# Triangular inverses from blocks of 8 instead of blocks of 16, with a product level from 8 to 16

## The chip, the cores and the metric

One core of a Trainium2 chip. The metric is the device time of one execution in microseconds. TensorE (PE) multiplies, VectorE (DVE), ScalarE (ACT) and GpSimd (POOL) work elementwise, SyncE (SP) issues most DMAs. Each engine works through its own queue in order.

## What is computed

Two layers of a recurrent decoder trunk on 1024 prompt rows and 8 x 8 sample rows of width 1024, in float32. Layer 0 mixes with an S5 scan and a gated DeltaNet (GDN, 4 heads of 128), layer 1 with RWKV-7 (16 heads of 64); each layer ends in a SwiGLU network of width 2816. What matters here is that GDN and RWKV are computed in chunks, and that each chunk needs the inverse of a unit triangular matrix:

```python
lmat = jnp.where(strict, jnp.einsum("nbhid,nbhjd->nbhij", k_beta, kb) * decay, 0.0)
eye = jnp.eye(CHUNK, dtype=jnp.float32)
tmat = lax.linalg.triangular_solve(eye + lmat, jnp.broadcast_to(eye, lmat.shape),
                                   left_side=True, lower=True)
...
state = (state * w_t[:, :, None, :] + sa[..., None] * b_t[:, :, None, :]
         + v_t[..., None] * k_t[:, :, None, :])
```

The RWKV recurrence is written step by step in the reference; the kernel computes it in chunks of 64, which brings in an inverse of the same kind.

## The kernel before, in words

The rows stand in the free dimension (1088 = 1024 + 64 columns), the features in the partitions. All large products go through `Kern.mm` (L293 to L302): operands are split into a high and a low part, and three products per 128 features are summed (`hi,wh`, `lo,wh`, `hi,wl`). `Kern.weight` (L280) loads a weight block as `raw`, casts it on ScalarE (`wh`, L289) and subtracts on GpSimd (`wl`, L290) or, in places, on VectorE. The feed-forward network (`Kern.ffn`, L456) makes products `pg` (gate and up) and `pd` (down); VectorE evicts them (L490, L496, L498, and L513, which adds to the residual `x`).

Between these dense products the program places the two recurrent mixers, which are made of small products and many elementwise steps:

- `GDN.segment` (L966): 4 heads, each in two segments, 8 calls. A call has 4 chunks of 128, the second segment also the 8 samples.
- `RWKV.unit` (L1517): 8 pairs of heads, each in 4 segments, 32 calls. A call has 4 chunks of 64 for two heads; the fourth segment a fifth for the samples.

Each call needs one batch of inverses, made by `Kern.inverse` (L141 to L257), 40 in all. It works in this order:

1. VectorE multiplies the 256 or 320 columns of the matrices with a mask (`mk`, L158) and adds up (`D`, L160), so that the 16x16 blocks on the diagonal stand next to each other. Two DMAs through DRAM (`dA`, L161 and L165) put each block into one partition (`L`).
2. Substitution: starting from the identity (`T`, L167), 15 steps of two instructions each, a product `Tm` (L172) and a subtraction or addition into `T` (L174), on 32 to 40 partitions and 15 to 64 elements.
3. Two DMAs (`dT`, L176 and L178) bring the inverted blocks back as columns `Tc`. A mask and a 32x32 transpose make `tt` and `t32` (L189, L194).
4. Level 16 to 32: two groups of 32x32 products with 16 columns, L202 and L206, with a ScalarE copy between (`Y`, L203) and a multiply-add at the end (L208), then a transpose (L212).
5. Level 32 to 64: two more groups (L230, L238) and copies; for GDN one more level from 64 to 128.

The order of the instructions on every engine is written by a scheduler that works from a model of its own when the program is built; the code gives data dependences and priorities. The units are thereby interleaved with dense products and with each other.

Of the kernel before, what the change touches and what calls it, by code (L numbers as in the profile page):

```python
# [8 lines left out]
F32 = mybir.dt.float32  # L9
# [3 lines left out]
OP = mybir.AluOpType  # L13
# [4 lines left out]
T = 1088  # L18
# [72 lines left out]
class Kern:  # L91
    def __init__(self, ctx, tc):
# [23 lines left out]
        def blocks(n, w, name):  # L116
# [7 lines left out]

        self.b16 = blocks(8, 16, "b16")
        self.b8 = blocks(16, 8, "b8")
        self.m4 = c.tile([128, 4], F32, name="m4")
        nc.vector.tensor_add(self.m4, self.b16[:, 0:4], self.b16[:, 4:8])
# [6 lines left out]
        ii = c.tile([128, 16, 16], F32, name="ii")  # L135
        nc.gpsimd.iota(ii, pattern=[[1, 16], [-1, 16]], base=0, channel_multiplier=0,
                       allow_small_or_imprecise_dtypes=True)
        nc.vector.tensor_scalar(ii, ii, 0.0, None, op0=OP.is_equal)
        self.i16 = ii

    def inverse(self, gp, ps, dr, A, wd, nu, ns, sgn, tag, pb=2, own=False, TT=None):  # L141

# [1 line left out]


        nc, v = self.nc, self.nc.vector
        nl = 8 * nu + ns
        op = OP.subtract if sgn > 0 else OP.add
        dA = dr.tile([nu + 1, 8, 256], F32, name="dA", tag="dA%d" % wd)
        size = {"mk": 320, "L": 256, "T": 256, "tt32": 160, "Y32": 160}  # L150
        kin = {"Y32": "L", "tt32": "T"}
        two = [lambda n, i=i: gp.tile([128, size[kin.get(n, n)] if own else 320], F32, name=n,
                                      tag="i" + kin.get(n, n) if own else "inv%d" % i, bufs=1) for i in range(2)]
        D = gp.tile([128, nu + 1, 16], F32, name="D", tag="invTc", bufs=1 + own)
        for R, n in ((slice(0, 64), nu + 1 if ns else nu), (slice(64, 128), nu)) if wd == 128 else ((slice(0, 128), nu),):
            mk = two[1]("mk").rearrange("p (u b i) -> p u b i", b=4, i=16)[R, 0:n]
# [4 lines left out]
        nc.sync.dma_start(dA[0:nu].rearrange("u b (j i) -> (b j) u i", i=16), D[:, 0:nu])  # L161
        if ns:
            nc.sync.dma_start(dA[nu, 0:ns].rearrange("b (j i) -> (b j) i", i=16), D[0:16 * ns, nu])
        L = two[0]("L")[:8 * nu + 8, :256].rearrange("p (a b) -> p a b", b=16)
        nc.sync.dma_start(L[:nl], dA.rearrange("u b (j i) -> (u b) j i", i=16)[:nl])  # L165
        T = two[1]("T")[:8 * nu + 8, :256].rearrange("p (a b) -> p a b", b=16)
        v.tensor_copy(T[:nl], self.i16[:nl])  # L167
        m = gp.tile([8 * nu + 8, 64], F32, name="Tm", tag="invm", bufs=1)
# [6 lines left out]
        dT = dr.tile([nu + 1, 8, 256], F32, name="dT", tag="dT%d" % wd)  # L175
        nc.sync.dma_start(dT.rearrange("u b x -> (u b) x")[:nl], T[:nl].rearrange("p c i -> p (c i)"))  # L176
        Tc = gp.tile([128, nu + 1, 16], F32, name="Tc", tag="invTc", bufs=1 + own)
        nc.sync.dma_start(Tc[:, 0:nu], dT[0:nu].rearrange("u b (c i) -> (b c) u i", i=16))  # L178
        TS = None
        if ns:  # L180
            R = 16 * ns
            nc.sync.dma_start(Tc[0:R, nu], dT[nu, 0:ns].rearrange("b (c i) -> (b c) i", i=16))
            TS = gp.tile([R, 4, 16], F32, name="TS", tag="invTS", bufs=1)
            v.tensor_mul(TS, Tc[0:R, nu:nu + 1].to_broadcast([R, 4, 16]),
                         self.m4[0:R, :, None].to_broadcast([R, 4, 16]))
            TS = TS.rearrange("p b i -> p (b i)")

        tt = gp.tile([128, nu, 2, 16], F32, name="tt", tag="invtt", bufs=1)
        v.tensor_mul(tt, Tc[:, 0:nu, None].to_broadcast([128, nu, 2, 16]),  # L189
                     self.half[:, None, :, None].to_broadcast([128, nu, 2, 16]))  # L190
        t32 = gp.tile([128, nu, 32], F32, name="t32", tag="invt32", bufs=1)
        fl = lambda x: x.rearrange("p u c -> p (u c)")
        tt = tt.rearrange("p u a i -> p u (a i)")
        v.transpose(fl(t32), fl(tt))  # L194
        Q = [slice(32 * b, 32 * b + 32) for b in range(4)]
        C = [slice(32 * b % wd, 32 * b % wd + 32) for b in range(4)]
        CT = Q
        Y = gp.tile([128, nu, 16], F32, name="Y16", tag="invY", bufs=1)
        py = ps.tile([128, 2, nu, 16], F32, tag=tag, name="py", bufs=pb)
        for u in range(nu):  # L200
# [6 lines left out]
        k = 1 if sgn > 0 else 0  # L207
# [977 lines left out]
class RWKV:  # L1185
# [32 lines left out]
    def consts(self, cp):  # L1218

        K, v = self.K, self.K.nc.vector  # L1220
        mk = cp.tile([128, 2, 64], F32, name="mk")
        for R in self.HR:
            v.tensor_scalar(mk[R, 0], K.iota[R, R], 0.0, None, op0=OP.is_gt)
            v.tensor_scalar(mk[R, 1], K.iota[R, R], 0.0, None, op0=OP.is_ge)
        self.mk = mk
        self.m8 = cp.tile([128, 8], F32, name="m8")
        v.tensor_add(self.m8, K.b8[:, 0:8], K.b8[:, 8:16])
# [850 lines left out]
```

## Time and profile before

| | us |
|---|---|
| median of 3 runs | 3781.07 (3778.25 to 3793.54) |
| the profiled execution's own time | 3776.02 |
| its span | 3774.2 |

The profile is of one execution. A row of the page or of a view gives an engine, a line of the kernel, the tile written and those read, and then busy time and mean duration, or a wait and what released it. Busy TensorE time includes matrix products whose ends are modelled. Products of full float32 operands leave two records each.

### The profile page before, as it was taken

What the parts mean: (1) busy time and instruction counts of PE and PEld (TensorE: products, weight loads), DVE (VectorE), ACT (ScalarE), POOL (GpSimd) and SP (SyncE); (2) the same over time, 40 slices, a digit from 0 to 9 for tenths busy, and PEclk for the clock granted to TensorE, in tenths of its full rate; (3) what the DMA queues carried; (4) which work ended last, traced back from release to release, by engine and by line L of the source; (5) the groups of instructions that cost most, each with busy time, mean ns of one, the idle gap of its engine ahead of it and who ended that gap; (6) DMA issues with size and microseconds to landing.
All of it is one profiled execution on the core that took longest, in us unless ns stands there. A gap on an engine that the chain in (4) does not pass through costs nothing. (4 is left out here: it accounts for less than half of the span.)

```text
span 3774.2 us, 77080 instructions
## 1 busy us (share of the span) xinstructions
PE 3475.1 (92%) x29894; PEld 3221.5 (85%) x29894; DVE 2512.1 (67%) x6836; ACT 1390.7 (37%) x3264; POOL 1317.6 (35%) x1189
## 2 busy tenths in 40 slices
PE   7889989999988889999999988898998999899998
PEld 6879888899978788888888877888888888799997
DVE  7876877654456477777777674577787877553444
ACT  3333433322225443434433354443443443232222
POOL 3322233222236543433333264543333333332221
PEclk9989997999988999999999988998998999899999
DMA  4424442322223552222222224721222322322222
GB/s 104 94 81 132 97 124 75 95 81 90 88 92 96 167 174 68 60 79 79 78 81 69 92 72 129 222 84 50 86 86 78 94 82 87 130 62 82 90 77 70
DMA packets 331405, 356.35 MB, mean 94 GB/s; under 512 B 133272, under 2 KB 273304, under 8 KB 331040
## 3 DMA queue, kind: packets, MB, share of 16 engines
q1 hardware_dynamic: 321824, 342.52, 30.7%
q10 hardware_dynamic: 9216, 8.92, 0.7%
q8 instruction: 235, 3.85, 0.4%
q14 instruction: 130, 1.06, 0.1%
HBM read 285.34 MB, written 64.81 MB: 93 GB/s over the span
## 5 line engine op out<-in xcount | busy, mean ns | idle before, releaser
L290 POOL TENSOR_TENSOR wl<-raw,wh 128x1024 fp32r<-128x1024 f32 (+2 forms) x301 | 701.7, 2333 | 1094.9 <-ACT wh L289 1018.1
L301 PE MATMUL pg<-hi,wh 128*128 128x288 f32 (+1 forms) x2816 | 841.0, 299 | 31.5 <-DVE s L490 17.8
L301 PE MATMUL pg<-lo,wh 128*128 128x288 f32 (+1 forms) x2816 | 836.9, 297 | 4.8 <-DVE lo L388 3.5
L301 PE MATMUL pg<-hi,wl 128*128 128x288 f32 (+1 forms) x2816 | 835.6, 297 | 0.0
L301 PEld LDWEIGHTS pg<-hi,wh 128*128 128x128 f32 x2816 | 544.4, 193 | 43.9 <-DVE s L490 20.5
L301 PEld LDWEIGHTS pg<-lo,wh 128*128 128x128 f32 x2816 | 544.4, 193 | 14.2 <-DVE lo L388 4.7
L301 PEld LDWEIGHTS pg<-hi,wl 128*128 128x128 f32 x2816 | 544.1, 193 | 4.9 <-issue 2.1
L289 ACT CAST wh<-raw 128x1024 fp32r<-128x1024 f32 (+3 forms) x309 | 312.6, 1013 | 355.9 <-PE pg L301 88.4
L301 PE MATMUL pd<-ah,wdh 128*128 128x256 f32 (+1 forms) x1280 | 388.2, 303 | 18.6 <-DVE x L513 17.2
L301 PE MATMUL pd<-ah,wdl 128*128 128x256 f32 (+1 forms) x1280 | 373.2, 292 | 1.4 <-POOL wdl L290 1.4
L301 PE MATMUL pd<-al,wdh 128*128 128x256 f32 (+1 forms) x1280 | 371.9, 291 | 0.0
L301 PEld LDWEIGHTS pd<-ah,wdh 128*128 128x128 f32 x1280 | 243.9, 191 | 30.0 <-DVE x L513 19.6
L301 PE MATMUL pj<-lo,wh 128*128 128x256 f32 (+1 forms) x768 | 240.3, 314 | 18.8 <-DVE lo L388 15.9
L301 PE MATMUL pj<-hi,wh 128*128 128x256 f32 (+1 forms) x768 | 239.5, 314 | 14.0 <-ACT hi L387 6.0
L301 PEld LDWEIGHTS pd<-ah,wdl 128*128 128x128 f32 x1280 | 243.8, 190 | 3.4 <-POOL wdl L290 1.7
L301 PEld LDWEIGHTS pd<-al,wdh 128*128 128x128 f32 x1280 | 244.2, 191 | 1.1 <-issue 0.8
L301 PE MATMUL pj<-hi,wl 128*128 128x256 f32 (+1 forms) x768 | 234.9, 308 | 1.5 <-POOL wl L290 1.4
L513 DVE TENSOR_TENSOR x<-x,pd 128x256 f32<-128x256 f32 (+1 forms) x384 | 163.4, 427 | 87.7 <-PE pd L301 82.5
L289 ACT CAST wdh<-raw 128x384 fp32r<-128x384 f32 (+1 forms) x224 | 111.3, 497 | 247.0 <-PE pd L301 170.6
L172 DVE TENSOR_TENSOR Tm<-L,T 32x15 f32<-32x15 f32 (+8 forms) x600 | 181.7, 303 | 28.6 <-DMA L<-dA 15.3
L174 DVE TENSOR_TENSOR T<-T,Tm 32x15 f32<-32x15 f32 (+8 forms) x600 | 190.6, 318 | 13.5
L301 PE MATMUL pi<-hi,wh 128*128 128x272 f32 x640 | 192.2, 300 | 4.0 <-ACT us L1788 2.5
(643 smaller groups left out, 8275.5 us busy)
## 6 DMA issues: line engine op xcount, KB each, us to landing
raw<-in_wg SPq DMA_DIRECT2D x88, 512.0 KB
raw<-in_wup SPq DMA_DIRECT2D x88, 512.0 KB
raw<-in_wd SPq DMA_DIRECT2D x192, 192.0 KB
raw<-in_win SPq DMA_DIRECT2D x20, 512.0 KB
raw<-pr ACTq DMA_DIRECT2D x64, 136.0 KB
raw<-in_wk SPq DMA_DIRECT2D x16, 512.0 KB
raw<-in_wr SPq DMA_DIRECT2D x16, 512.0 KB
raw<-in_wv SPq DMA_DIRECT2D x16, 512.0 KB
```

The costliest lines, as they stand in the source:

```text
L172: v.tensor_mul(mm, L[:nl, j:j + 1, j + 1:16].to_broadcast([nl, j + 1, n]), T[:nl, 0:j + 1, j:j + 1].to_broadcast([nl, j + 1, n]))
L174: v.tensor_tensor(T[:nl, 0:j + 1, j + 1:16], T[:nl, 0:j + 1, j + 1:16], mm, op=op)
L289: nc.scalar.copy(wh, raw)
L290: (lo or nc.gpsimd).tensor_sub(wl, raw, wh)
L301: self.nc.tensor.matmul(ps, a[k], b[:, c:c + cn], start=i == 0, stop=i == last)
L513: v.tensor_add(x[m][:, c:c + cn], x[m][:, c:c + cn], ps)
```

## The change

The blocks that are inverted by substitution are 8x8 instead of 16x16. There are twice as many, in twice as many partitions (64 to 80); the substitution has 7 steps instead of 15, on 7 to 16 elements. A new level from 8 to 16 stands ahead of the old one from 16 to 32: the same two groups of 32x32 products with 16 columns, a ScalarE copy between them, two multiply-adds out of PSUM and one more transpose. Four masks are made differently at the start of the program. The DMAs are as many as before, with half the bytes. In `RWKV.consts` one mask is taken over instead of computed.

```diff
-        nl = 8 * nu + ns
+        nl = 16 * nu + 2 * ns
...
-            v.tensor_mul(mk, A[R, 0:n, c0:c0 + 64].rearrange("p u (b i) -> p u b i", i=16),
-                         self.m4[R, None, :, None].to_broadcast([R.stop - R.start, n, 4, 16]))
+            v.tensor_mul(mk, A[R, 0:n, c0:c0 + 64].rearrange("p u (b i) -> p u b i", i=8),
+                         self.m8[R, None, :, None].to_broadcast([R.stop - R.start, n, 8, 8]))
...
-        for j in range(15):
-            n = 15 - j
+        for j in range(7):
+            n = 7 - j
             mm = m[:nl, :(j + 1) * n].rearrange("p (c i) -> p c i", i=n)
-            v.tensor_mul(mm, L[:nl, j:j + 1, j + 1:16].to_broadcast([nl, j + 1, n]),
+            v.tensor_mul(mm, L[:nl, j:j + 1, j + 1:8].to_broadcast([nl, j + 1, n]),
                          T[:nl, 0:j + 1, j:j + 1].to_broadcast([nl, j + 1, n]))
-            v.tensor_tensor(T[:nl, 0:j + 1, j + 1:16], T[:nl, 0:j + 1, j + 1:16], mm, op=op)
+            v.tensor_tensor(T[:nl, 0:j + 1, j + 1:8], T[:nl, 0:j + 1, j + 1:8], mm, op=op)
...
+        tt = gp.tile([128, nu, 4, 8], F32, name="tt8", tag="invtt8", bufs=1)
+        v.tensor_mul(tt, Tc[:, 0:nu, None].to_broadcast([128, nu, 4, 8]),
+                     self.q8[:, None, :, None].to_broadcast([128, nu, 4, 8]))
+        tt = tt.rearrange("p u a i -> p u (a i)")
+        t32 = gp.tile([128, nu, 32], F32, name="t32", tag="invt32", bufs=1)
+        v.transpose(fl(t32), fl(tt))
+        te = t32.rearrange("p u (a i) -> p u a i", i=16)[:, :, :, 0:8]
+        Y = gp.tile([128, nu, 16], F32, name="Y8", tag="invY", bufs=1)
+        py = ps.tile([128, 2, nu, 16], F32, tag=tag, name="py0", bufs=pb)
+        for u in range(nu):
+            for b in range(4):
+                nc.tensor.matmul(py[Q[b], 0, u].rearrange("p (a i) -> p a i", i=8), A[Q[b], u, C[b]], te[Q[b], u],
+                                 start=True, stop=True)
+        nc.scalar.copy(Y, py[:, 0])
+        for u in range(nu):
+            for b in range(4):
+                nc.tensor.matmul(py[Q[b], 1, u], tt[Q[b], u], Y[Q[b], u], start=True, stop=True)
+        for a in range(2):
+            v.scalar_tensor_tensor(te[:, :, a], py[:, 1, :, 8 * a:8 * a + 8], self.odd8[:, k, a:a + 1], te[:, :, a],
+                                   op0=OP.mult, op1=OP.add)
+        tt = gp.tile([128, nu, 32], F32, name="tt", tag="invtt", bufs=1)
+        v.transpose(fl(tt), fl(t32))
```

The scheduler lays every queue out anew. On VectorE, in an RWKV unit of the second mixed stretch, the end of one substitution and the steps behind it stand like this before (a row has the line, the operation, the tile written and those read, and its shape; `XV` and `X` belong to the unit before, `s` and `al` to the feed-forward network):

```order
L172 TENSOR_TENSOR Tm<-L,T 32x39
L174 TENSOR_TENSOR T<-T,Tm 32x13x3
L172 TENSOR_TENSOR Tm<-L,T 32x28
L1656 COPY X<-pc 64x64
L174 TENSOR_TENSOR T<-T,Tm 32x14x2
L172 TENSOR_TENSOR Tm<-L,T 32x15
L490 SCALAR_TENSOR_TENSOR s<-s,pg 128x288
L174 TENSOR_TENSOR T<-T,Tm 32x15
L1659 COPY XV<-pc 64x64
L496 TENSOR_TENSOR s<-s,pg 128x288
L189 TENSOR_TENSOR tt<-Tc,half 128x128
L194 STREAM_TRANSPOSE t_18439<-tt 128x128
```

and with the change (lines are 21 or 22 higher there for the same code further down; L177 and L179 are the substitution):

```order
L179 TENSOR_TENSOR T<-T,Tm 64x6x2
L177 TENSOR_TENSOR Tm<-L,T 64x7
L179 TENSOR_TENSOR T<-T,Tm 64x7
L518 TENSOR_TENSOR s<-s,pg 128x288
L520 SCALAR_TENSOR_TENSOR al<-s,ah 128x288
L1680 COPY XV<-pc 64x64
L512 SCALAR_TENSOR_TENSOR s<-s,pg 128x288
L199 TENSOR_TENSOR tt_18445<-Tc,q_87 128x128
L203 STREAM_TRANSPOSE t_18447<-tt_18445 128x128
```

Seven pairs stand where fifteen stood, and four instructions instead of two stand between the last of them and the mask product that needs the columns back from DRAM.

On TensorE, in the third stretch, the 31st inverse has these two groups before (with 18 dense products `pd` between the last row of the first and the first row of the second piece, left out):

```order
L202 MATMUL py<-t_31527,MB 32x16 x13
L1652 MATMUL pc<-XV,AR 128x128
L202 MATMUL py<-t_31527,MB 32x16
L1668 MATMUL py<-H,Q 64x64
L202 MATMUL py<-t_31527,MB 32x16 x2
...
L206 MATMUL py<-Y_31529,tt 32x16 x9
L1657 MATMUL pc<-X,TT_13298 128x64
L206 MATMUL py<-Y_31529,tt 32x16 x7
```

and with the change these four (with 20, 22 and 20 dense products `pg` left out between them):

```order
L209 MATMUL py_32207<-t_32204,MB 32x16 x8
...
L214 MATMUL py_32207<-Y_32206,tt_32202 32x16
L1689 MATMUL py<-H,Q 64x64
L214 MATMUL py_32207<-Y_32206,tt_32202 32x16 x15
...
L225 MATMUL py<-t_32204,MB 32x16 x14
L1690 MATMUL py<-XV,BG 64x64
L225 MATMUL py<-t_32204,MB 32x16 x2
...
L229 MATMUL py<-Y_32245,tt 32x16 x8
```

The two new groups have the form of the old ones and stand ahead of them, each some 20 dense products after the group before. Counted over the whole order, 19104 dense products stand in it before and after; between the first and the last inverse of the second mixed stretch it has 3233 of them before and 3137 with the change, in the third stretch 3339 and 3135.

## Rows read from the trace of the kernel before

**Rows 1.** The page: busy time of two engines over the span.

```profile
PE 3475.1 (92%) x29894; PEld 3221.5 (85%) x29894; DVE 2512.1 (67%) x6836; ACT 1390.7 (37%) x3264; POOL 1317.6 (35%) x1189
```

**Rows 2.** Windows of four stretches: length, busy by engine (instructions), PE clock, DMA.

```profile
300.00:850.00 550.00, 518.08 (x4559) 482.65 (x4558) 402.76 (x1218) 187.59 (x390) 156.46 (x140) 0.92 0.35 98
1360.00:2110.00 750.00, 707.41 (x6450) 646.21 (x6449) 565.93 (x1695) 304.65 (x806) 265.63 (x251) 0.97 0.26 75
2425.00:3190.00 765.00, 714.30 (x7078) 639.99 (x7076) 594.54 (x1791) 310.62 (x839) 282.90 (x264) 0.95 0.28 81
3400.00:3700.00 300.00, 300.00 (x2260) 300.00 (x2260) 120.94 (x216) 79.18 (x136) 76.83 (x32) 1.00 0.27 83
```

**Rows 3.** Waits of TensorE (us, times, longest): 300:850; 1360:2110; then three of 2425:3190.

```profile
PE pg L301 <- DVE lo L388: 3.5, 2, 3.3
...
PE pc L1652 <- DVE XV L1663: 11.6, 11, 1.9
...
PE pg L301 <- DVE s L490: 10.0, 5, 4.0
...
PE py L202 <- DVE t L194: 2.6, 3, 1.9
...
PE pc L1652 <- DVE H L1663: 0.2, 1, 0.2
```

**Rows 4.** Chain of waits in the third stretch, shares of it by line.

```profile
by line: PE pg L301 23.7%; PE pd L301 8.2%; DVE Tm L172 5.7%; DVE T L174 4.6%; issue 3.5%; PE pg L1620 2.5%; DVE BK L1587 2.3%; PE po L301 2.2%; DMA rkb<-dks 2.0%; PE pc L1660 1.9%; PE py L1669 1.8%; DVE x L513 1.5%; PE pn L1739 1.4%; PE py
```

**Rows 5.** Windows of the third stretch: busy time of line L172, then of L174.

```profile
2425.00:3190.00 765.00, 76.12 (x240) 0.95 0.28 81
...
2425.00:3190.00 765.00, 75.70 (x240) 0.95 0.28 81
```

**Rows 6.** The page's groups: busy us, mean ns, idle before.

```profile
L172 DVE TENSOR_TENSOR Tm<-L,T 32x15 f32<-32x15 f32 (+8 forms) x600 | 181.7, 303 | 28.6 <-DMA L<-dA 15.3
L174 DVE TENSOR_TENSOR T<-T,Tm 32x15 f32<-32x15 f32 (+8 forms) x600 | 190.6, 318 | 13.5
```

**Rows 7.** Groups by shape in the first stretch, 300 to 850 us.

```profile
L172 DVE TENSOR_TENSOR Tm<-L,T 32x15 f32<-32x15 f32 x8 | 1.3, 162 | 2.4 <-DMA L<-dA 2.4
L174 DVE TENSOR_TENSOR T<-T,Tm 32x64 f32<-32x64 f32 x4 | 0.8, 212 | 0.1
```

**Rows 8.** Timeline from 2437 us, VectorE, then GpSimd: start us, us.

```profile
2438.05 1.87 DVE L172 TENSOR_TENSOR Tm<-L,T 32x64 f32<-32x64 f32 x1
...
2437.45 2.40 POOL L290 TENSOR_TENSOR wl<-raw,wh 128x1024 fp32r<-128x1024 f32 x1 [3.60 <-ACT wh L289]
```

**Rows 9.** Groups by line, whole span: the other steps of the inverse.

```profile
L167 DVE COPY T<-ii 32x256 f32<-32x256 f32 (+2 forms) x40 | 19.5, 487 | 0.6
L189 DVE TENSOR_TENSOR tt<-Tc,half 128x128 f32<-128x128 f32 (+1 forms) x40 | 14.8, 371 | 62.3 <-DMA Tc<-dT 62.3
L212 DVE STREAM_TRANSPOSE tt<-t 128x128 f32<-128x128 f32 (+1 forms) x40 | 12.5, 313 | 0.6
L208 DVE SCALAR_TENSOR_TENSOR t<-py,odd,t 128x64 f32<-128x64 f32 (+1 forms) x40 | 11.2, 280 | 5.4 <-PE py L206 4.9
L203 ACT COPY Y<-py 128x64 f32<-128x64 f32 (+1 forms) x40 | 8.5, 214 | 21.7 <-PE py L202 21.0
```

**Rows 10.** Windows, sum over the three stretches, of line L202, then of L206.

```profile
sum 2065.00, PE 25.04 PEld 18.25; mean PE 8.35 PEld 6.08
...
sum 2065.00, PE 22.03 PEld 16.53; mean PE 7.34 PEld 5.51
```

**Rows 11.** Timeline of TensorE around one L206 group: start us, us.

```profile
2454.11 0.29 PE L301 MATMUL pj<-lo,wh 128*128 128x288 f32 x1
2454.33 0.44 PE L206 MATMUL py<-Y,tt 32*32 32x16 f32 x32
2454.70 0.40 PE L301 MATMUL pj<-hi,wl 128*128 128x288 f32 x1
2454.94 0.30 PE L301 MATMUL pj<-hi,wh 128*128 128x288 f32 x1
```

More of the change, by code (lines that the diff above doesn't have):

```diff
@@ L126, in __init__ @@
         self.b8 = blocks(16, 8, "b8")
-        self.m4 = c.tile([128, 4], F32, name="m4")
-        nc.vector.tensor_add(self.m4, self.b16[:, 0:4], self.b16[:, 4:8])
+        self.m8 = c.tile([128, 8], F32, name="m8")
+        nc.vector.tensor_add(self.m8, self.b8[:, 0:8], self.b8[:, 8:16])
+        self.q8 = c.tile([128, 4], F32, name="q8")
+        nc.vector.tensor_add(self.q8, self.m8[:, 0:4], self.m8[:, 4:8])
+        self.odd8 = c.tile([128, 2, 2], F32, name="odd8")
+        for i, f in enumerate((1.0, -1.0)):
+            nc.vector.tensor_scalar(self.odd8[:, i], self.q8[:, 1:4:2], f, None, op0=OP.mult)
         self.half = c.tile([128, 2], F32, name="half")
@@ L133, in __init__ @@
         nc.vector.tensor_scalar(self.odd[:, 1:2], self.half[:, 1:2], -1.0, None, op0=OP.mult)
-        ii = c.tile([128, 16, 16], F32, name="ii")
-        nc.gpsimd.iota(ii, pattern=[[1, 16], [-1, 16]], base=0, channel_multiplier=0,
+        ii = c.tile([128, 8, 8], F32, name="ii")
+        nc.gpsimd.iota(ii, pattern=[[1, 8], [-1, 8]], base=0, channel_multiplier=0,
                        allow_small_or_imprecise_dtypes=True)
         nc.vector.tensor_scalar(ii, ii, 0.0, None, op0=OP.is_equal)
-        self.i16 = ii
+        self.i8 = ii
@@ L141, in inverse @@
     def inverse(self, gp, ps, dr, A, wd, nu, ns, sgn, tag, pb=2, own=False, TT=None):
         nc, v = self.nc, self.nc.vector
-        nl = 8 * nu + ns
+        nl = 16 * nu + 2 * ns
         op = OP.subtract if sgn > 0 else OP.add
-        dA = dr.tile([nu + 1, 8, 256], F32, name="dA", tag="dA%d" % wd)
-        size = {"mk": 320, "L": 256, "T": 256, "tt32": 160, "Y32": 160}
+        dA = dr.tile([nu + 1, 16, 64], F32, name="dA", tag="dA%d" % wd)
         kin = {"Y32": "L", "tt32": "T"}
-        two = [lambda n, i=i: gp.tile([128, size[kin.get(n, n)] if own else 320], F32, name=n,
+        two = [lambda n, i=i: gp.tile([128, {"mk": 320}.get(n, 160) if own else 320], F32, name=n,
@@ L153, in inverse @@
                                       tag="i" + kin.get(n, n) if own else "inv%d" % i, bufs=1) for i in range(2)]
-        D = gp.tile([128, nu + 1, 16], F32, name="D", tag="invTc", bufs=1 + own)
+        D = gp.tile([128, nu + 1, 8], F32, name="D", tag="invTc", bufs=1 + own)
         for R, n in ((slice(0, 64), nu + 1 if ns else nu), (slice(64, 128), nu)) if wd == 128 else ((slice(0, 128), nu),):
-            mk = two[1]("mk").rearrange("p (u b i) -> p u b i", b=4, i=16)[R, 0:n]
+            mk = two[1]("mk").rearrange("p (u b i) -> p u b i", b=8, i=8)[R, 0:n]
@@ L162, in inverse @@
         if ns:
[L163 to L168, printed above, removed]
-        for j in range(15):
-            n = 15 - j
+            nc.sync.dma_start(dA[nu, 0:2 * ns].rearrange("b (j i) -> (b j) i", i=8), D[0:16 * ns, nu])
@@ L171, in inverse @@
+        L = two[0]("L")[:16 * nu + 16, :64].rearrange("p (a b) -> p a b", b=8)
+        nc.sync.dma_start(L[:nl], dA.rearrange("u b (j i) -> (u b) j i", i=8)[:nl])
+        T = two[1]("T")[:16 * nu + 16, :64].rearrange("p (a b) -> p a b", b=8)
+        v.tensor_copy(T[:nl], self.i8[:nl])
+        m = gp.tile([16 * nu + 16, 16], F32, name="Tm", tag="invm", bufs=1)
+        for j in range(7):
+            n = 7 - j
             mm = m[:nl, :(j + 1) * n].rearrange("p (c i) -> p c i", i=n)
-            v.tensor_mul(mm, L[:nl, j:j + 1, j + 1:16].to_broadcast([nl, j + 1, n]),
+            v.tensor_mul(mm, L[:nl, j:j + 1, j + 1:8].to_broadcast([nl, j + 1, n]),
@@ L173, in inverse @@
                          T[:nl, 0:j + 1, j:j + 1].to_broadcast([nl, j + 1, n]))
-            v.tensor_tensor(T[:nl, 0:j + 1, j + 1:16], T[:nl, 0:j + 1, j + 1:16], mm, op=op)
-        dT = dr.tile([nu + 1, 8, 256], F32, name="dT", tag="dT%d" % wd)
+            v.tensor_tensor(T[:nl, 0:j + 1, j + 1:8], T[:nl, 0:j + 1, j + 1:8], mm, op=op)
+        dT = dr.tile([nu + 1, 16, 64], F32, name="dT", tag="dT%d" % wd)
         nc.sync.dma_start(dT.rearrange("u b x -> (u b) x")[:nl], T[:nl].rearrange("p c i -> p (c i)"))
-        Tc = gp.tile([128, nu + 1, 16], F32, name="Tc", tag="invTc", bufs=1 + own)
@@ L178, in inverse @@
-        nc.sync.dma_start(Tc[:, 0:nu], dT[0:nu].rearrange("u b (c i) -> (b c) u i", i=16))
+        Tc = gp.tile([128, nu + 1, 8], F32, name="Tc", tag="invTc", bufs=1 + own)
+        nc.sync.dma_start(Tc[:, 0:nu], dT[0:nu].rearrange("u b (c i) -> (b c) u i", i=8))
         TS = None
@@ L181, in inverse @@
             R = 16 * ns
[L182 to L185, printed above, removed]
+            nc.sync.dma_start(Tc[0:R, nu], dT[nu, 0:2 * ns].rearrange("b (c i) -> (b c) i", i=8))
+            TS = gp.tile([R, 8, 8], F32, name="TS", tag="invTS", bufs=1)
+            v.tensor_mul(TS, Tc[0:R, nu:nu + 1].to_broadcast([R, 8, 8]),
+                         self.m8[0:R, :, None].to_broadcast([R, 8, 8]))
             TS = TS.rearrange("p b i -> p (b i)")
[L188 to L191, printed above, removed]
         fl = lambda x: x.rearrange("p u c -> p (u c)")
-        tt = tt.rearrange("p u a i -> p u (a i)")
-        v.transpose(fl(t32), fl(tt))
         Q = [slice(32 * b, 32 * b + 32) for b in range(4)]
@@ L1225, in consts @@
         self.mk = mk
-        self.m8 = cp.tile([128, 8], F32, name="m8")
-        v.tensor_add(self.m8, K.b8[:, 0:8], K.b8[:, 8:16])
+        self.m8 = K.m8
         self.mks = cp.tile([128, 2, 64], F32, name="mks")
```

4 lines of the change are left out of this document (2 added, 2 removed).

## The prediction

> **What bounds the kernel now.** I read the page first: TensorE is busy 92% of the span, VectorE 67% [rows 1]. That alone would condemn a change that moves work from VectorE to TensorE, so the next view is the one by stretch. The 40 inverses lie in three mixed stretches, 300 to 850 (GDN), 1360 to 2110 and 2425 to 3190 us (RWKV units between dense products), and there TensorE is not full: of 550, 750 and 765 us it is busy 518, 707 and 714, so it idles 32, 43 and 51 us; its granted clock is 0.92, 0.97 and 0.95. In a purely dense stretch, 3400 to 3700, it is full at clock 1.00 [rows 2]. In the mixed stretches VectorE is busy 73 to 78%.
>
> For whom TensorE idles there is in the waits: in the third stretch 18 kinds of wait are released by VectorE and sum to 45 us, from `s L490` with 10.0 down to `H L1663` with 0.2 [rows 3]. The first and second stretch have 16 and 13 such kinds with 22 and 36 us, led by 3.5 and 11.6 us [rows 3]. Together 103 us of TensorE's 125 us of idle time wait for VectorE. Almost none of these wait for the inverse itself; they wait for an eviction that is queued behind other VectorE work.
>
> The chain shows what that work is: over the third stretch the substitution's two lines are 5.7% and 4.6% of it, 10.3% of 765 = 79 us [rows 4], while their busy time there is 76 + 76 = 152 us [rows 5]. So 52% of the substitution lies on the path in that stretch.
>
> **What the change takes from VectorE.** One inverse issues 15 pairs of instructions now and 7 after. Their total busy time is 181.7 + 190.6 = 372 us for 40 inverses [rows 6], 9.3 us each. Undisturbed, an instruction takes 162 ns at 15 elements and 212 at 64 [rows 7], some 147 ns plus 1.02 ns an element. The old sizes sum to 680 elements, which gives 2 x (15 x 0.147 + 0.69) = 5.8 us; the new ones (7, 12, 15, 16, 15, 12, 7) sum to 84, which gives 2.2 us. The rest of the 9.3 is waiting: the 64-element product at 2438.05 took 1.87 us instead of 0.21 [rows 7, 8], and ended within 0.1 us of GpSimd's 2.40 us subtraction that began at 2437.45 [rows 8].
>
> So the saving has two ends. If only undisturbed time goes, it is 5.8 - 2.2 = 3.6 us, 143 us over 40. If the waits shrink in proportion, it is 9.3 x (1 - 2.2/5.8) = 5.8 us, some 230 us.
>
> The Trainium skill has a rule on that wait, in "SBUF — State Buffer", section "Who interferes with whom": a VectorE instruction with two SBUF inputs contends with a GpSimd instruction that reads SBUF, and whoever started first holds the port for its whole instruction. The rows just quoted agree: the wait ended with GpSimd's instruction. Read strictly the rule speaks against the change, since the length of a wait is GpSimd's and passes to the next VectorE instruction of that kind; the sum by it is the lower end, 143.
>
> Smaller things on VectorE: the start copy of the identity goes from 256 to 64 elements; it costs 0.49 us now [rows 9], and I take 0.25 off, -10 us in all (0 to -14). The mask product and its reduction still read 256 elements: nothing. Added per inverse are a second transpose (0.31) and two multiply-adds out of PSUM of half the size of one that takes 0.28 [rows 9]; at 0.25 each that is 0.8 us, +32 us in all. VectorE's net relief is then between 143 + 10 - 32 = 121 and 230 + 10 - 32 = 208 us. I take 165, the middle.
>
> **What it puts on TensorE.** The new level has the same two groups of 32x32 products with 16 columns as the level from 16 to 32. Those two lines are busy 25.0 and 22.0 us in the three stretches, 1344 records each [rows 10]; a copy of them is 47 us. A single place confirms it: between the dense product at 2454.11 and the second one after the group, at 2454.94, lie 0.83 us where two dense steps of 0.13 would be 0.27, so a group of 16 displaces 0.56 us [rows 11]. There are 84 groups' worth (1344 records at two per product, 16 products to a group, two lines), and 84 x 0.56 = 47. No cover hides this: TensorE is the engine that ends last, so all 47 us count.
>
> **Hand-offs, DMA, ScalarE.** Per inverse two more groups wait on other engines. The order puts about 20 dense products ahead of each, 20 x 0.13 = 2.6 us, so I cost them at nothing; were that cover gone, the present wait of `py L202`, 2.6 us over 16 inverses [rows 3], doubled and taken over 40, would be +13. ScalarE gains 40 copies of 0.21 us [rows 9], 9 us on an engine that is busy 34 to 41% [rows 2]: nothing. The number of transfers and queue issues on SP is unchanged, their pieces are half as long (32 bytes for the columns, twice the lanes with rows of 256 bytes). VectorE now waits 62 us in all for the columns to come back [rows 9]; I leave that as it is, with ±20 us of VectorE time for the range, so ±10 on the path.
>
> **The sum.** At 52% on the path, VectorE's relief is worth 63 to 108 us, 85 in the middle; but it can only be had as TensorE idle time, of which 103 us wait for VectorE. The order also spends part of it: it packs the units closer (over the third stretch's 16 units it has 3135 dense products instead of 3339, over the second's 3137 instead of 3233), so the margins ahead of the evictions do not grow by all that VectorE gains. I take 70, nearer the lower end, since the one wait that I could follow ends with GpSimd's instruction and not with VectorE's. The net is 47 - 70 = -23 us on the profiled execution's 3776.0, or 3753. The median of the runs, 3781.1, is 5 us above that execution, so on that scale the forecast is **3758 us**, 0.6% faster. A measurement of this kernel can tell about 0.5%, 19 us, from no change, so this is only just outside.
>
> **The rivals.**
> 1. *TensorE simply gets more to do: slower.* Place: the unit streams of the two RWKV stretches, where TensorE already runs at 94%. The 47 us are paid in full and, because the closer order spends VectorE's gain, the same evictions are late as before. The price is +47 less what little returns, say 10: 3818. It decides as soon as less than 28 us of the 103 come back (47 - 28 = 19). For it: 92% busy, and that the waits are many and short. Against it: 52% of the substitution on the chain. Chance 0.22.
> 2. *GpSimd's waits move on: no change.* VectorE is rid of 121 us only, and the instructions that come next inherit the waits. At 52% that is 63, and with the closer order some 45 to 60 come back: 47 - 50 = -3, so 3778. The place of [rows 8] is for it; against it is that an eviction out of PSUM, such as `x L513`, was not seen held up like that. Chance 0.33, together with the part of the forecast that falls within 19 us. By the port rule of the Trainium skill ("SBUF — State Buffer", section "Who interferes with whom"), read strictly, this is the outcome.
> 3. *The clock comes too: much faster.* Granted clocks of 0.92, 0.97 and 0.95 mean 88, 45 and 76 us at 1.2 GHz instead of 2.4, about 105 us of lost TensorE time. If all 103 us of waits and a third of that loss came back, the net is 47 - 103 - 35 = -91: 3690. Against it: no row ties these slow spells to the inverses. Chance 0.10, inside "faster".
> 4. *The change does not do what it says.* The order excludes it: 7 pairs, two new groups, both multiply-adds.
>
> **How the numbers follow.** My forecast and rival 3 have 0.45 together above 0.5% faster, rival 2 and the forecast's near side 0.33, rival 1 0.22. The range reaches from 3705 (nearly all waits, little clock) to 3815 (nearly all of rival 1 with a hand-off or two late). The likeliest case's own range is 3733 to 3783 (returns of 45 to 95 us).
>
> **What would show it.** Right: substitution lines with 280 instructions each and in sum 90 to 145 us instead of 372; two new lines of small products with 45 to 50 us; VectorE busy 2300 to 2400 us instead of 2512; TensorE idle in the mixed stretches down from 125 us to about 60. Wrong: idle of 100 us or more with the evictions still on top of the waits (rival 1), or a substitution instruction whose mean stays near 310 ns while other two-input lines grow (rival 2). I would be wrong in kind if a wait for the returning columns or for the new products led the list.

## Result and profile after

The median went from 3781.07 to 3811.99 us (five executions of each, 3778.25 to 3793.54 and 3807.51 to 3832.84). The ratio, worked out from all executions, is 1.0089, 95% interval 1.0064 to 1.0114 (the two medians alone give 1.0082): 0.9% slower, 54 us above the forecast of 3758 and 3 us below the upper end of the range. The profiled execution of the changed kernel is the slowest of its five, 3832.84 us with a span of 3831.0; it was granted a clock of 0.934, and the four others had 0.939 to 0.943 and took 3807.5 to 3818.3. That of the kernel before had 0.941. So TensorE's busy time after the change holds some 20 us that go with the clock (change_nudge_one below, nearly the same kernel at 0.940, has 3534.0 instead of 3553.3).

The page's busy line, answering [rows 1]:

```profile
PE 3553.3 (93%) x32582; PEld 3285.7 (86%) x32582; DVE 2372.5 (62%) x6318; ACT 1403.6 (37%) x3304; POOL 1305.5 (34%) x1189
```

VectorE has 139.6 us less to do, TensorE 78 us more, and TensorE's idle time over the whole span (span less busy) is 277.7 us where it was 299.1. The windows of the three mixed stretches (columns as in [rows 2]) say where:

```profile
300.00:880.00 580.00, 552.87 (x5130) 512.36 (x5129) 389.85 (x1117) 189.69 (x401) 148.57 (x141) 0.90 0.33 93
1395.00:2170.00 775.00, 741.12 (x7516) 674.88 (x7516) 513.33 (x1489) 313.31 (x829) 260.82 (x246) 0.95 0.25 71
2480.00:3260.00 780.00, 741.56 (x8371) 660.81 (x8370) 527.85 (x1628) 321.60 (x881) 285.67 (x269) 0.96 0.28 81
```

The stretches are 580, 775 and 780 us long in place of 550, 750 and 765, and TensorE idles 27, 34 and 38 us in them in place of 32, 43 and 51. So 26 us of idle time came back, where the prediction had 70, against 47 of new products.

The groups by line on VectorE, answering [rows 6, 9] (columns: busy us, mean ns of one, idle before):

```profile
L520 DVE SCALAR_TENSOR_TENSOR al<-s,ah 128x288 fp32r<-128x288 f32 (+1 forms) x176 | 158.5, 900 | 67.9 <-ACT ah L519 67.3
L177 DVE TENSOR_TENSOR Tm<-L,T 64x7 f32<-64x7 f32 (+11 forms) x280 | 72.0, 257 | 32.5 <-DMA L<-dA 27.1
L179 DVE TENSOR_TENSOR T<-T,Tm 64x7 f32<-64x7 f32 (+11 forms) x280 | 67.5, 241 | 5.8
L1608 DVE SCALAR_TENSOR_TENSOR BK<-ta,Pi 64x256 f32<-64x256 f32 (+1 forms) x64 | 51.6, 807 | 2.6 <-PE pt L1630 1.8
L1613 DVE SCALAR_TENSOR_TENSOR r<-r,rvec,kp 128x256 f32<-128x256 f32 (+1 forms) x32 | 30.4, 949 | 0.1
L199 DVE TENSOR_TENSOR tt<-Tc,q 128x128 f32<-128x128 f32 (+1 forms) x40 | 23.0, 574 | 60.7 <-DMA Tc<-dT 60.6
L172 DVE COPY T<-ii 64x64 f32<-64x64 f32 (+2 forms) x40 | 17.5, 437 | 0.6
L216 DVE SCALAR_TENSOR_TENSOR t<-py,odd,t 128x32 f32<-128x32 f32 (+1 forms) x80 | 16.4, 245 | 10.7 <-PE py L214 9.4 <-ACT XV L1680 0.8
L219 DVE STREAM_TRANSPOSE tt<-t 128x128 f32<-128x128 f32 (+1 forms) x40 | 12.6, 316 | 1.0
```

The substitution takes 139.5 us in place of 372: the upper of the two ends. But the net relief is not what follows from it. 233 for the substitution and 2 for the copy, less 29 for the new multiply-adds and the transpose, is 206; measured are 140. The rest sits in lines that the change does not touch, or whose amount of work it leaves alone. The same groups in the kernel before:

```profile
L498 DVE SCALAR_TENSOR_TENSOR al<-s,ah 128x288 fp32r<-128x288 f32 (+1 forms) x176 | 132.7, 754 | 63.5 <-ACT ah L497 62.4 <-DMA raw<-in_wg 0.5
L1587 DVE SCALAR_TENSOR_TENSOR BK<-ta,Pi 64x256 f32<-64x256 f32 (+1 forms) x64 | 45.1, 704 | 4.3 <-PE pt L1609 3.8
L1592 DVE SCALAR_TENSOR_TENSOR r<-r,rvec,kp 128x256 f32<-128x256 f32 (+1 forms) x32 | 24.3, 760 | 0.4
```

`al` grew by 25.8 us, `BK` by 6.5, `r` by 6.1, and the mask product behind the returning columns from 14.8 to 23.0, each with as many instructions of the same shape. That is 47 of the 66. Part of it belongs to the order and not to the relief: `al`, which is busy 132.7 us before, takes 145 to 147 in level_added, groups_twice and groups_one, where the substitution is the old one, and 155 to 167 in relief_only, change_no_loop and no_substitution, while `BK` and `r` are shorter than before in some of these kernels and longer in others.

On TensorE the windows over the three stretches (the sum alone, as in [rows 10]) of the two new lines, L209 and then L214, show what was forecast, 26.9 + 23.4 = 50 us:

```profile
sum 2135.00, PE 26.86 PEld 19.11; mean PE 8.95 PEld 6.37
...
sum 2135.00, PE 23.41 PEld 17.31; mean PE 7.80 PEld 5.77
```

The chain of waits in the third stretch, answering [rows 4]:

```profile
by line: PE pg L323 22.8%; PE pd L323 7.4%; PE po L323 3.7%; DVE BK L1608 3.0%; DVE Tm L177 2.9%; DMA rkb<-dks 2.7%; issue 2.7%; PE pg L1641 2.6%; PE py L1690 2.2%; PE pc L1681 2.1%; DMA dT<-T 2.1%; DMA Tc<-dT 2.1%; DVE T L179 2.0%; PE pj L
```

The substitution's share fell from 10.3% of 765 us, 79, to 4.9% of 780, 38. 41 us left the chain, and the stretch did not get shorter: `BK`, `rkb`, the two transfers of the columns and `po` have larger shares.

### The profile page after: what moved, and what is told of

It reads as the page before. It is cut to its first block, busy times and chain, and to the rows that moved or that the text cites. A ratio compares the mean times of both kernels' runs of the same rounds, so it can differ in the third digit from the quotient of the medians.

```text
span 3831.0 us, 82110 instructions
## 1 busy us (share of the span) xinstructions
PE 3553.3 (93%) x32582; PEld 3285.7 (86%) x32582; DVE 2372.5 (62%) x6318; ACT 1403.6 (37%) x3304; POOL 1305.5 (34%) x1189
## 5 line engine op out<-in xcount | busy, mean ns | idle before, releaser
L323 PE MATMUL pj<-hi,wh 128*128 128x256 f32 (+1 forms) x768 | 242.1, 317 | 15.3 <-ACT hi L409 6.0
L520 DVE SCALAR_TENSOR_TENSOR al<-s,ah 128x288 fp32r<-128x288 f32 (+1 forms) x176 | 158.5, 900 | 67.9 <-ACT ah L519 67.3
L312 POOL TENSOR_TENSOR wdl<-raw,wdh 128x384 fp32r<-128x384 f32 (+1 forms) x112 | 111.6, 996 | 241.5 <-ACT wdh L311 214.2
```

The source lines that it names most:

```text
L312: (lo or nc.gpsimd).tensor_sub(wl, raw, wh)
L323: self.nc.tensor.matmul(ps, a[k], b[:, c:c + cn], start=i == 0, stop=i == last)
L520: v.scalar_tensor_tensor(al[:, c:c + cn], t, 0.5, ah[:, c:c + cn], op0=OP.mult, op1=OP.subtract)
```

## Experiments

Theories at the start. **A**: TensorE pays for its products in full, and VectorE's relief returns only some 20 to 30 us. **B**: the products are not the cost but the new hand-offs between TensorE, ScalarE and VectorE. **C**: the relief is worth nothing since the waits behind GpSimd pass to other instructions. After the first four runs a theory **D** went further than A: it offers a reason why the relief returns so little, and is put in the expectations of the runs that follow.

All results, with the profiled execution's busy times. Idle is the span less TensorE's busy time. The ratio is to executions of the kernel before taken beside each run.

| kernel | median us | ratio to before, 95% | VectorE busy | TensorE busy | TensorE idle | clock |
|---|---|---|---|---|---|---|
| before | 3781.07 | | 2512.1 | 3475.1 | 299.1 | 0.941 |
| the change | 3811.99 | 1.0089 (1.0064 to 1.0114) | 2372.5 | 3553.3 | 277.7 | 0.934 |
| level_added | 3854.70 | 1.0186 (1.0169 to 1.0202) | 2517.8 | 3537.8 | 312.4 | 0.940 |
| relief_only | 3780.81 | 0.9986 (0.9973 to 0.9999) | 2342.4 | 3487.3 | 293.2 | 0.938 |
| groups_twice | 3836.71 | 1.0138 (1.0118 to 1.0158) | 2510.4 | 3523.7 | 313.3 | 0.936 |
| gdn_only | 3790.29 | 1.0013 (1.0004 to 1.0023) | 2491.7 | 3489.3 | 299.0 | 0.942 |
| no_substitution | 3767.01 | 0.9961 (0.9946 to 0.9976) | 2254.6 | 3496.8 | 277.3 | 0.934 |
| substitution_twice | 3968.09 | 1.0496 (1.0477 to 1.0516) | 2743.5 | 3567.0 | 407.0 | 0.912 |
| change_no_loop | 3776.50 | 0.9984 (0.9967 to 1.0001) | 2256.0 | 3517.3 | 262.3 | 0.942 |
| rwkv_only | 3795.52 | 1.0037 (1.0022 to 1.0051) | 2387.5 | 3507.4 | 291.0 | 0.944 |
| groups_one | 3763.05 | 0.9958 (0.9943 to 0.9973) | 2507.0 | 3447.7 | 309.9 | 0.939 |
| new_level_one | 3787.75 | 1.0021 (1.0005 to 1.0037) | 2382.7 | 3487.8 | 299.5 | 0.944 |
| before_nudge_one | 3782.58 | 1.0003 (0.9986 to 1.0019) | 2505.7 | 3481.2 | 303.2 | 0.941 |
| change_nudge_one | 3814.64 | 1.0088 (1.0068 to 1.0107) | 2374.9 | 3534.0 | 283.3 | 0.940 |

The kernel before had a median of 3784.34 us beside the first four, 3781.33 beside the second and 3781.02 beside the third.

### The two halves of the change apart

**level_added**: the kernel before, with the whole new level added and its result multiplied by 0.

```diff
+        for u in range(nu):
+            for b in range(4):
+                nc.tensor.matmul(py[Q[b], 0, u]..., A[Q[b], u, C[b]], te[Q[b], u], start=True, stop=True)
+        nc.scalar.copy(Y, py[:, 0])
+        for u in range(nu):
+            for b in range(4):
+                nc.tensor.matmul(py[Q[b], 1, u], tt[Q[b], u], Y[Q[b], u], start=True, stop=True)
+        for a in range(2):
+            v.scalar_tensor_tensor(te[:, :, a], py[:, 1, ...], self.nil[:, a:a + 1], te[:, :, a], ...)
+        v.transpose(fl(tt), fl(t32))
```

> The kernel before, with the whole new level added behind its 15-step substitution: the same two groups of products, the ScalarE copy, two multiply-adds (with a factor of 0, so the values stay) and a second transpose. Theory A (TensorE pays): the 47 us of products count in full, and 33 us more work on VectorE add up to 10: 3781 + 47 to 57 = 3828 to 3838. Theory C (the relief of VectorE is worth nothing because GpSimd's waits move on): the level alone costs what the whole change costs, +31: about 3812.

**relief_only**: the change without its new level; blocks of 8, 7 steps, everything else.

```diff
-        for u in range(nu):
-            for b in range(4):
-                nc.tensor.matmul(py[Q[b], 0, u].rearrange("p (a i) -> p a i", i=8), A[Q[b], u, C[b]], te[Q[b], u],
...
-        for a in range(2):
-            v.scalar_tensor_tensor(te[:, :, a], py[:, 1, :, 8 * a:8 * a + 8], self.odd8[:, k, a:a + 1], te[:, :, a],
...
-        v.transpose(fl(tt), fl(t32))
```

> The changed kernel without its new level: the products from 8 to 16, their copy, the multiply-adds and the second transpose are left out, so the blocks of 16 stay block-diagonal; the 7-step substitution on blocks of 8 stays. Theory A: TensorE's work is as before, and VectorE's relief returns about 20 to 30 us of its idle time: 3750 to 3762. Theory C: nothing comes back: 3775 to 3785. My prediction's own value was 70 back: 3711.

**groups_twice**: the kernel before with the products of L202 and L206 issued twice, nothing that waits is added.

```diff
-        for u in range(nu):
+        for u in list(range(nu)) * 2:
```

> The kernel before, with each of the two groups of products of the level from 16 to 32 issued twice in a row; no new wait, no new VectorE or ScalarE work. Theory A: 35 to 47 us more, 3816 to 3828. Theory B (the new hand-offs between the engines cost, not the products): 0 to 10 us more, 3781 to 3791.

**gdn_only**: the change in GDN's 8 inverses, the old inverse in RWKV's 32.

```diff
-        TT, _ = K.inverse(gp, self.ps, self.dr, MB, 64, C, 0, -1.0, "qi", 1, True, self.TT[self.turn])
+        TT, _ = K.inverse16(gp, self.ps, self.dr, MB, 64, C, 0, -1.0, "qi", 1, True, self.TT[self.turn])
```

> The change in the 8 inverses of GDN alone; the 32 of RWKV are made as before. Theory A: a fifth of the cost, 9 us of products less about 4 that come back: 3781 + 5, 3777 to 3790. If the loss sat in the GDN stretch, where the profile after shows granted clocks of 0.81 and 0.77 between 500 and 700 us, it would be nearly the whole +31: 3800 to 3812.

The relief alone, 170 us of VectorE, gives 0.14%, some 5 us. The products alone, 47 us without one new hand-off, cost 1.38%, 52 us. The level alone costs 70. So B falls: the larger part of what the level costs is there without its hand-offs. My 70 us for the relief fall too, and so do the 20 to 30 us of A; the 3780.8 lie where C had them, but C had 3812 for level_added, which measured 3854.7, and A had no more than 3838. But -5 and +70 make 65 and not the 31 of the change: the relief is worth 39 us where the level is, and 5 where it is not.

One place to look at is the end of the third stretch. There the output projection `po` stands behind two things: by its data behind the last unit (its output `yo`), and in TensorE's queue behind the last dense product `pd` of the feed-forward network and the norm that follows it. The trace by line and by tile gives the first and the last start in us. In relief_only, `yo`, then the last `pd`, then `po`:

```profile
L1703 DVE SCALAR_TENSOR_TENSOR yo<-pT,rvec,bv x32: 468/484/551, 1473.2 to 3209.0; 128x256 f32<-128x256 f32 x24, 128x320 f32<-128x320 f32 x8
...
L306 PE MATMUL pd<-ah,wl x32: 274/282/580, 3223.0 to 3245.0; 128*128 128x256 f32 x32
...
L306 PE MATMUL po<-hi,wh x128: 288/295/588, 3261.1 to 3315.4; 128*128 128x288 f32 x128
```

The same three in the kernel before:

```profile
L1699 DVE SCALAR_TENSOR_TENSOR yo<-pT,rvec,bv x32: 461/484/551, 1464.4 to 3244.5; 128x256 f32<-128x256 f32 x24, 128x320 f32<-128x320 f32 x8
...
L301 PE MATMUL pd<-ah,wl x32: 278/283/416, 3211.3 to 3237.9; 128*128 128x256 f32 x32
...
L301 PE MATMUL po<-hi,wh x128: 288/296/588, 3254.4 to 3309.1; 128*128 128x288 f32 x128
```

What `po` waits for in the kernel before stands in TensorE's timeline (start us, us):

```profile
3252.70 1.94 PE L355 MATMUL bc<-rst,selq 128*128 128x64 f32 x8 [4.37 <-DVE rst L321]
3254.40 0.59 PE L301 MATMUL po<-hi,wh 128*128 128x288 f32 x1
```

`po` starts right behind the last products of the norm (`bc`), 10 us after the last `yo`. The relief brings the last unit in 35 us earlier (3209.0 for 3244.5), and `po` no earlier, since it starts 16 us after the last `pd`: 3237.9 to 3254.4 before, 3245.0 to 3261.1 with the relief. In level_added it is the other way: the last `yo` starts at 3333.9, after `po` has begun at 3306.8, and the `po` products are spread over 78 us instead of 55. That is one place where the new level costs more than its products. This was theory D: the units run inside a stream of dense TensorE work, both must be through, and in the kernel before the dense stream is the one that is waited for. At this place the traces bear it out.

They do not show it to be the reason why the relief returns so little, for the dense stream itself could have come earlier. All kernels have the same 19104 dense products in nearly the same order, so a stretch can be measured from one dense product to another, the same two in both kernels. Here are the first and the third stretch (columns as in [rows 2]), in one execution of the kernel before and then in one of relief_only:

```profile
300.11:850.03 549.92, 518.00 (x4558) 482.57 (x4557) 402.65 (x1218) 187.59 (x390) 156.46 (x140) 0.92 0.35 98
2425.11:3320.04 894.93, 822.33 (x8077) 739.16 (x8075) 670.87 (x1995) 348.20 (x924) 326.35 (x297) 0.94 0.29 87
```

```profile
296.34:867.81 571.47, 525.41 (x4559) 487.31 (x4557) 384.56 (x1089) 187.20 (x390) 150.81 (x140) 0.92 0.34 93
2453.03:3326.37 873.34, 815.73 (x8076) 733.64 (x8075) 590.06 (x1739) 347.76 (x924) 327.69 (x297) 0.95 0.30 88
```

With the same products on TensorE, the third stretch is 22 us shorter for 81 us less of VectorE, and the first is 22 us longer for 18 us less, with TensorE idle 46 us instead of 32. So the relief does pay in the third stretch, and the 5 us are what is left after another stretch lost as much. Why the first one lost it no run shows; it is part of the order, which moves the stretches in before_nudge_one too (below: +9 us in the first, -9 in the third, for one instruction on one element per inverse). The change has no one place for its loss either: by the same measure it is 23 us longer in the first stretch, 30 in the time that goes from 1360 to 2425 us before and holds the second, and 1 in the third; change_nudge_one has 21, 13 and 13.

### How much relief and load are worth

**no_substitution** and **substitution_twice**, on the kernel before:

```diff
-        for j in range(15):
+        for j in range(0):
```

```diff
-        v.tensor_copy(T[:nl], self.i16[:nl])
...
-        for j in range(15):
+        for j in [*range(15), *range(15)]:
+            if j == 0:
+                v.tensor_copy(T[:nl], self.i16[:nl])
```

> The kernel before without its 15-step substitution loop, in all 40 inverses: T stays the identity, so the substitution is left out of the computation. It takes 372 us of VectorE (two lines of 600 instructions) out, more than twice the change's relief, and nothing of TensorE. Theory D (TensorE's own stream sets the time: the units run inside a dense stream of TensorE work, the stretch ends when both are through, and in the kernel before the units end just ahead of the dense stream, so a relief of VectorE has almost nothing left to shorten): 3755 to 3780 us, 0 to 25 us faster, TensorE's idle time behind VectorE falls by no more than 25 us. The prediction's view (52% of the waits chain is VectorE, TensorE idles 103 us behind it, and a relief gives this back up to that cap): 3680 to 3710 us. Theory C (the waits move on to GpSimd): no faster than 3770 us, and TensorE's idle time behind GpSimd rises by what is lost behind VectorE.

> The kernel before with the substitution loop run twice from a fresh identity (the first result is overwritten): 372 us of VectorE and 40 copies more, in the chain of every unit, nothing more on TensorE, the same result. Theory D: the units of the second half, which in the kernel before end just ahead of the dense stream, now end behind it, and each further us of a unit's chain counts from there: 60 to 200 us slower (3845 to 3980), several times what leaving the loop out gives. The prediction's view (a share of the chain that pays in both directions): as much slower as no_substitution is faster, some 70 to 100 us (3850 to 3880). If VectorE's load does not count at all: 3785 us.

**change_no_loop**, on the change:

```diff
-        for j in range(7):
+        for j in range(0):
```

> The change without its 7-step loop (the substitution is left out of the computation): 139.5 us of VectorE less than the change, TensorE as in the change. Theory D: the products of the new level are paid in full and the relief has nothing left to give: 3795 to 3815 us, 0 to 15 us below the change, and still 15 to 35 us above the kernel before although VectorE has some 280 us less to do than there. The prediction's view: a further 52% of 139.5, capped by the 83 us that TensorE still idles behind VectorE: 3740 to 3760 us.

**rwkv_only**, the counterpart of gdn_only:

```diff
-        TT, TS = K.inverse(alt, self.ps, self.dr, A, 128, 4, 4 if s else 0, 1.0, tag, 1)
+        TT, TS = K.inverse16(alt, self.ps, self.dr, A, 128, 4, 4 if s else 0, 1.0, tag, 1)
```

> The change in RWKV's 32 inverses only; GDN's 8 keep blocks of 16. 38 of the 47 us of new TensorE work. With gdn_only at plus 0.13% (5 us) and the whole change at plus 0.89% (34 us): if the two parts add, 3805 to 3815 us (plus 0.6 to 0.85%). If GDN's part only seems cheap because another stretch hides it, and costs 10 us or more beside RWKV's: 3795 to 3803. Theory D gives the first.

Taking the substitution out altogether gives 0.39%, 14 us of its 372 (VectorE's busy time falls by 258, since other lines grow). Putting it in once more costs 4.96%, 187 us, half of 372. That this half is near the prediction's share of 52% confirms nothing: VectorE's busy time rose by 231 us and not by 372, and of the 200 us between the two profiled spans 108 are idle time of TensorE and 92 are its busy time, for the same 29894 products, at a clock of 0.912 instead of 0.941. The busy lines of the two pages:

```profile
PE 3496.8 (93%) x29894; PEld 3242.4 (86%) x29894; DVE 2254.6 (60%) x5636; ACT 1394.1 (37%) x3264; POOL 1308.9 (35%) x1189
```

```profile
PE 3567.0 (90%) x29894; PEld 3285.5 (83%) x29894; DVE 2743.5 (69%) x8076; ACT 1395.8 (35%) x3264; POOL 1329.9 (33%) x1189
```

With VectorE at 60% TensorE still idles 277 us, 22 less than before, and its busy time is 22 more for the same products, at a clock of 0.934 in this execution. Over all its executions no_substitution was granted 0.938 on average, the kernel before beside it 0.942; why less, no run shows, but it takes back a part of the relief. C's sign is missing: TensorE's waits behind GpSimd are 7.9 us over the whole span where they were 9.4. The list of TensorE's waits in no_substitution shows why my cap of 103 us was no reserve: many short waits behind the same evictions, some shorter than before and some longer (22.4, 6.0, 15.3 and 15.9 us are what the list of the kernel before has for these four).

```profile
PE pd L301 <- DVE x L513: 16.3, 17, 3.4
PE py L1669 <- DVE XV L1659: 16.0, 14, 2.9
PE py L819 <- DVE Z L779: 15.4, 2, 9.6
PE pj L301 <- DVE lo L388: 13.8, 10, 2.3
```

In substitution_twice the units run past the dense stream:

```profile
L1700 DVE SCALAR_TENSOR_TENSOR yo<-pT,rvec,bv x32: 461/483/552, 1508.7 to 3459.0; 128x256 f32<-128x256 f32 x24, 128x320 f32<-128x320 f32 x8
...
L302 PE MATMUL po<-hi,wh x128: 288/295/609, 3335.4 to 3509.6; 128*128 128x288 f32 x128
```

The last unit comes 124 us after the first `po`. The order shows what else changed. Counted from the first to the last unit's product `pu` (`pc<-X,TT` in a trace), it holds 3443 dense products in the third stretch before, 3487 in substitution_twice and 3522 in level_added, but 3334 in the change, 3333 in no_substitution and 3295 in relief_only: in this stretch the scheduler gives each unit fewer dense products between its steps when VectorE has less to do. That suggests that part of what VectorE gains goes into ending the units earlier and not into margins before the evictions; how many us that cost is not shown. Nor is it a general rule: groups_twice has 3341 here with VectorE's work unchanged, and in the second stretch relief_only has 3438 for 3420 before.

D did not hold everywhere. change_no_loop came out at 3776.5, 35 us below the change, where D had 0 to 15 (and the prediction's view 52 to 72). TensorE idled 262 us there, the least of all. With the level in the kernel, relief is worth over a quarter of what VectorE's busy time falls by (39 us for 145 from level_added to the change, 35 for 116 from there on); without it 3 to 5% (5 for 170, 14 for 258). That the longer units of the level are nearer to being the last is in line with level_added, but in the change they already end 24 us ahead of the last `pd` (3272.7 and 3296.5), so it does not explain the second step, and this stays open. Read the other way round, the level with its 47 to 50 us of products costs 1.86% (70 us) beside 15 steps, 1.03% (39) beside 7 and 0.23% (9) beside none: TensorE's new work is not always paid in full, which A, D and the prediction all took for granted. The two parts of the change do not add either: 0.13% (gdn_only) and 0.37% (rwkv_only) make 0.50% of 0.89%; 15 us are not assigned to either.

### TensorE's share, and the order's

**groups_one**, on the kernel before, and **new_level_one**, on the change:

```diff
-        for u in range(nu):
-            for b in range(4):
-                nc.tensor.matmul(py[Q[b], 0, u], A[Q[b], u, C[b]], t32[Q[b], u, 0:16], start=True, stop=True)
+        nc.tensor.matmul(py[:, 0], fl(A[:, 0:128 // wd]), t32[:, :, 0:16], start=True, stop=True)
...
-        for u in range(nu):
-            for b in range(4):
-                nc.tensor.matmul(py[Q[b], 1, u], tt[Q[b], u], Y[Q[b], u], start=True, stop=True)
+        nc.tensor.matmul(py[:, 1], fl(tt[:, 0:4]), Y, start=True, stop=True)
```

> The kernel before with each of the two groups of the level from 16 to 32 issued as one 128x128 product with 64 columns in place of 16 products of 32x32; so the level's result is left out (blocks are mixed). TensorE has some 84 x 0.45 = 38 us less to do, VectorE and the hand-offs are untouched. Theory D (TensorE's own work is what counts, VectorE's load hardly does): 20 to 40 us faster, 3740 to 3762, for a tenth of the work whose removal on VectorE (372 us) gave 14. Lower end if the units, which are not shortened by this, now end last. The prediction's view turned round (TensorE idles anyway behind VectorE, so less TensorE work becomes more idle time): under 15 us faster, 3766 or more.

> The change, with each of the two groups of the new level issued as one 128x128 product (the new level's result is left out). All of the change's relief, its hand-offs, its two multiply-adds and its transpose stay; only 38 of the 47 us of its new TensorE work go. Theory D: 20 to 40 us below the change, 3770 to 3795, that is about the kernel before. If the hand-offs of the new level were what costs (theory B): no more than 10 us below the change, 3800 to 3815.

**before_nudge_one** and **change_nudge_one**:

```diff
+        for i in range(1):
+            v.tensor_scalar(T[:nl, 0, 0:1], T[:nl, 0, 0:1], 1.0, None, op0=OP.mult)
         dT = dr.tile([nu + 1, ...
```

> The kernel before with one more VectorE instruction on one element at the end of each substitution (a product with 1.0, same result): 40 x 0.15 = 6 us of VectorE, enough for the scheduler to lay out another order. It shows how much a new order alone moves the time: theory D has 0 to 6 us for the work (3781 to 3787). A difference of 15 us or more in either direction would mean that single comparisons under 0.5% here tell of the order and not of the edit.

> The change with the same one-element instruction at the end of each substitution. Same purpose, and the change once more on another day in another order: 3806 to 3822 us by theory D, plus 0.7 to 1.1% against the kernel before. At 3795 or less, part of the change's loss is the luck of its order.

groups_one is 0.42% faster, 18 us. It takes 27 us of TensorE's busy time (3447.7 for 3475.1, at clocks of 0.939 and 0.941) and leaves idle 11 us longer. That is just under what D had and above the other view's 15. Some 27 us of TensorE are thus worth about as much as 372 of VectorE (0.42% and 0.39%). new_level_one is the cleanest comparison with the change: relief, hand-offs, multiply-adds and transpose all stay, the products go, and 24 of the change's 31 us go with them. The nudges show that an order laid out anew moves the whole time of these kernels by little, though it moves single stretches: +0.03% before, and the change again at +0.88% in another order. So the loss is not the luck of one order; nor is it the clock, for the executions of change_nudge_one were granted 0.942 on average, as were those of the kernel before beside them.

## Why the prediction was wrong

- *New work on TensorE, 47 us, all of it counts*: right in size, the two lines measured 50 us. In the kernel before, the same number of products without hand-offs cost 52; beside the short substitution the whole level costs 39, and beside none 9. That all of it counts is thus near enough for the change, and not a rule.
- *Substitution 143 to 230 us less*: right at the upper end, 233 measured. The copy of the identity gave 2 us, not 10: its median went from 282 to 186 ns as taken, but a few copies of up to 2.7 us carry the mean (up to 2.4 before).
- *VectorE's net relief 165*: 140 measured, since `al`, `BK`, `r` and the mask product grew by 47 us. The Trainium skill's rule ("SBUF — State Buffer", section "Who interferes with whom") has a two-input VectorE instruction wait for a GpSimd instruction that holds the port. In its strict reading the wait passes on; its end was 143 of substitution and 121 net. The traces lie between: the substitution lost its waits nearly in proportion, 90 us beyond those 143, and other two-input instructions grew by 47. That these are the same waits passed on is not shown; only `al` grew in every kernel with less substitution, and by 12 to 15 us in three kernels with the old one. Rival 2 was right that other lines would grow, but it is not what decided.
- *52% of the relief lies on the path, capped by 103 us of waits, "I take 70"*: this is the step that failed. About 26 us came back in the profile of the change, and alone, without the level, 170 us of relief gave 5 and leaving out all 372 gave 14. The chain's 52% is where the substitution lay, not what a shorter one gives: 41 us of substitution left the chain of the third stretch and other work took their place. The 103 us were waits of TensorE behind VectorE, but for the most part not behind VectorE's load: with VectorE at 60% such waits are 181 us over the whole span where they were 200. Why so little came back is known in part only: in relief_only one stretch gained 22 us and another lost 22.
- I saw that the order packs the units closer (3135 dense products for 3339) and took 15 us off for it, though no run says what it is worth; no run here isolates it.
- *Hand-offs at nothing*: about right. new_level_one has them all and lies 7 us above the kernel before, so some 10 to 13 above relief_only; that still holds two larger products per inverse, the multiply-adds and the transpose.
- *Rival 1* comes nearest: the price was put at 47 less 10, 3818, against 3812 measured. Its condition, less than 28 us back, was met with 26; its place, the RWKV stretches alone, was not, since the first stretch lost 23 us too. It had 0.22; the sign of "92% busy, the waits many and short" should have weighed more than the chain's share. The clock of rival 3 brought nothing: 0.90, 0.95 and 0.96 in the three stretches where it was 0.92, 0.97 and 0.95.

## What to carry to other kernels

Where one engine is over 90% busy and the work beside it is interleaved by a scheduler, price a change first by what it does to that engine, and take idle time behind another engine as regained only when an experiment without the cost shows it: here the relief alone (5 us), or leaving the step out altogether (14), would have decided it. A share of the chain of waits says where a step lies, not what less of it gives: other work takes its place, so look for the second stream that must be through at the same place, and by how much it is behind. And take the time apart by stretches, between the same two dense products in both kernels: a sum near zero can be a gain and a loss.

No kernel here that leaves nothing out is faster than the one before. Since even no substitution at all gains 14 us, a cheaper one on VectorE has little to give in this kernel; fewer products in the inverse have as much (18 us for one level).

## What the runs showed of the hardware

- The time of one and the same program follows the clock that was granted: the change took 3833 us at 0.934, 3818 at 0.939 and 3808 at 0.943, some 3 us for each 0.001. A profiled execution 21 us above the median goes with that, and busy times of TensorE are to be compared with the clock beside them.
- Slow instructions of VectorE are few and long here, not all a little longer. The first line of the substitution after the change, by line (minimum, median and maximum in ns), has a median of 164 where the mean is 257:

```profile
L177 DVE TENSOR_TENSOR Tm<-L,T x280: 135/164/3070, 343.1 to 3193.6; 64x7 f32<-64x7 f32 x28, 64x15 f32<-64x15 f32 x28, 64x12 f32<-64x12 f32 x28, 64x16 f32<-64x16 f32 x14
```

- One 128x128 product of 64 columns in place of sixteen 32x32 products of 16 (groups_one) took 27 us off TensorE's busy time over 84 groups' worth, 0.33 us a group, where I had worked out 0.45. The clock was 0.939 for 0.941, so the true figure is somewhat higher.
